# The shared expert's products move into the first routed block, and the rest of it into a later one

## The chip, the cores and the metric

The kernel runs on one core of a Trainium2 chip. The metric is the device time of one execution in microseconds, the median of several runs. The core has five engines that run side by side and are tied by semaphores: TensorE (PE, the matrix products), VectorE (DVE), ScalarE (ACT), GpSimd (POOL) and SyncE (SP), which here issues the DMAs that bring the weights from memory.

## The reference

One decoder layer for 256 tokens of width 1024. The first half (a convolution branch, an attention branch and an output projection) is not touched by the change. The second half is a mixture of experts: 64 routed experts of which each token uses 8, and one shared expert that every token uses.

```
def moe_ffn(h, w_router, router_bias, w_gu, w_down, w_sh_gu, w_sh_down):
    t = h.reshape(B * S, D)
    scores = jax.nn.sigmoid((t @ w_router).astype(f32))
    ...                                     # top 8 of 64, limited to 4 of 8 groups -> gates
        g, u = jnp.split(jnp.einsum('td,edf->tef', tc, w_gu), 2, axis=-1)
        return jnp.einsum('tef,efd->td', jax.nn.silu(g) * u * gc[..., None], w_down)
    ...
    sg, su = jnp.split(t @ w_sh_gu, 2, axis=-1)
    shared = (jax.nn.silu(sg) * su) @ w_sh_down
    return (routed + shared).reshape(B, S, D)
```

Everything is float32. An expert has a gate/up matrix of 1024 x 512 (2 MB) and a down matrix of 256 x 1024 (1 MB).

## The kernel before

**Blocks.** The routed experts are computed in blocks of 128 slots. Blocks 0, 1 and 2 take two fixed experts each, 64 slots for an expert; all later blocks take experts in the order of how many tokens chose them (the ranked blocks), with 1, 2 or 4 experts in a block. Tokens are gathered into a block's slots by products with a selection matrix (`moves`, L1523), and scattered back by products with its transpose (`combine`, L1710).

**One block on the engines.** In `experts` (L1790): 16 gate/up products (L1802; 32 with four experts in a block), silu on ScalarE (L1672), gating on VectorE (L1676), which also needs the gate column that VectorE makes from a small product (L1564, L1577), two transposes on TensorE (L1823), their copy on ScalarE (L1685), and the down products (L1849). VectorE scales their result (L1694), and it is scattered back a block later. ScalarE's first silu of a block needs the table of silu, which `activate` asks for when it comes to it; the table before it is that of the sigmoid.

**The shared expert.** `shared` (L1768) multiplies the two halves of the tokens, t = 0 and 1, with the shared gate/up matrix, 2 products for each of 8 row blocks k (L1784), first k = 0 to 3 for both halves (q = 0), then 4 to 7 (q = 1). Once the first routed block is prepared (the event `blk 0`) it stops until the event `static`, which block 3 sets after its gate/up products. When a half is complete, `shared_tail` (L1635) applies silu and the gating, two transposes (L1625), a copy (L1629) and the down products in two halves (L1647), scaled by VectorE (L1650) and added by GpSimd (L1653).

**The overflow chain.** `overflow` (L1443) finds the experts with more tokens than slots: small products (L1446, L1447, L1455, L1461, L1462) that go back and forth between TensorE and VectorE, then two transposes (L1474), a copy and products (L1479). Its list is read by every engine at the end (L1947); it is put into SP's queue as early as it fits.

**What sets the order.** All this is written as generators (fibers) which a planner (`Plan`, L49) runs while the kernel is built. Each `yield` names an engine and a cost, an event, or a buffer of a pool; the planner keeps a clock for each engine and lets that fiber go next that can start first, and of equals the one with the higher number in `PRIO` (L25). `shared`, `shared_tail` and `overflow` have 0 and fill what others leave. The result is one fixed order of instructions on each engine; at run time only semaphores decide when each starts. A change of one event can so move many instructions.

**The weights.** All loads are issued by SP, strictly in the order of `todo` (L252). A load needs a buffer of 1 MB (`fa` or `late_w`) and is put into the queue where the planner expects that buffer to be free; on the chip SP then waits for the products that last read it. The two down matrices of block 2 are in `late_w`; their buffers go to two of the four down matrices of block 3. The loads before these take the buffers of block 0 (in halves), of block 1 and of block 2's gate/up matrices.

Of the kernel before, what the change touches and what calls it, by code (L numbers as in the profile page):

```python
# [13 lines left out]
AF = mybir.ActivationFunctionType  # L14
# [173 lines left out]
def AP(n, table=None):  # L188
    return "A", 0.06 + 0.00082 * n, table
# [11 lines left out]
def tile_hybrid_block(ctx, tc, x, c, positions, w_ada, b_ada, norm1_g, w_in, conv_dw, conv_dw_b,  # L201
# [3 lines left out]
    nc = tc.nc  # L205
# [1280 lines left out]
    def evacuate(xt, f, p, p3, ns, b0):  # L1486
        for f2 in range(2):
            k = f + f2
            e = yield TS(ns) if not b0 and f % 4 == 0 else AP(ns)
            if e == "A":  # L1490
                nc.scalar.activation(xt[:, k, 0:ns], p3[:, f2, 0:ns], AF.Identity, bias=b2c[:, k:k + 1],  # L1491
                                     scale=a2c[:, k:k + 1])
            else:
                nc.vector.tensor_scalar(xt[:, k, 0:ns], p3[:, f2, 0:ns], a2c[:, k:k + 1], b2c[:, k:k + 1],
                                        op0=OP.mult, op1=OP.add)
        pl.put("bank", p)
        pl.set("xt", b0, f // 2)
# [90 lines left out]
    def gathers():  # L1588
        tables[0] = yield Get("pm")
        held = []  # L1590
        for t in range(2):
            pl.cur.prio = PRIO["gathers" if t else "compare"]
            yield pl.ev("rx", t)
            yield from compare(0, t, rxp[0])
            for q in range(2):
                yield pl.ev("xr", t, q)
            if t:
                pl.set("first_pm")
                opened(0, (yield Get("xt")))
            for f in range(0, K, 2):  # L1600
                if not t:
                    held.append((yield Get("bank")))
                yield MM(4 * 2 * P)
                p3 = moved(0, held[f // 2], f, (t,))
                if t:
                    pl.spawn(evacuate(pl.events["info", 0].whole, f, held[f // 2], p3, 2 * P, 0))
        for b in range(2):
            pl.set("blk", b)
        for b in range(2):
            yield from slots(b)  # L1610
# [22 lines left out]
    shared_left = [2]  # L1633

    def shared_tail(t, pg):  # L1635
        aT = yield from gate_up(pg, None)
        yield pl.ev("L", "sd", 0, 0)
        wd = loaded["sd", 0]
        yield max(wd.at)
        for i in (10, 11):  # L1640
            yield pl.ev("ada", i)
        for h in range(2):
            d = slice(h * 512, (h + 1) * 512)
            pd = yield Get("bank")
            yield MM(8 * 512)
            for f in range(2):
                nc.tensor.matmul(pd, aT[:, f], wd.k[f][:, d], start=(f == 0), stop=(f == 1))  # L1647
            tm = yield Get("tm2")
            yield TT(512)
            nc.vector.tensor_tensor(tm, pd, g2b[:, d], op=OP.mult)  # L1650
            pl.put("bank", pd)
            e = yield [GT(512), TT(512) + (None, 1.0)]
            (nc.gpsimd if e == "G" else nc.vector).tensor_tensor(x_sb[:, t, d], x_sb[:, t, d], tm, op=OP.add)  # L1653
            pl.put("tm2", tm)
        pl.put("aT", aT)
        shared_left[0] -= 1
        if not shared_left[0]:
            done(("sd", 0), 0)
            pl.put("o32", *(fa(80 + 2 * i, 512) for i in range(2)))
            pl.set("shared")  # L1660
# [107 lines left out]
    def shared():  # L1768
        w = None
        pgs = []  # L1770
        for q in range(2):
            for t in range(2):
                for k in range(4 * q, 4 * q + 4):
                    yield pl.ev("h2", t, k)
                    if not k:
                        pgs.append((yield Get("bank")))
                    yield pl.ev("L", "sg", 0, k // 2)
                    w = loaded["sg", 0]
                    yield w.at[k]
                    if pl.ev("blk", 0).t is not None:  # L1780
                        yield pl.ev("static")
                    for c_ in (slice(0, 256), slice(256, 512)):
                        yield MM(4 * 256)
                        nc.tensor.matmul(pgs[t][:, c_], h2T[:, k, t * P:(t + 1) * P], w.k[k][:, c_],  # L1784
                                         start=(k + c_.start == 0), stop=(k == K - 1 and c_.start > 0))
                if q:
                    pl.spawn(shared_tail(t, pgs[t]))
            done(("sg", 0), q)

    def experts():  # L1790
        for b, (kd, js) in enumerate(blocks):
# [53 lines left out]
            for f in range(2):  # L1845
                for h in range(2):
                    yield "P", 0.87
                    for e, o, m in tiles_of[kd]:
                        nc.tensor.matmul(pd[h][o:o + m], info.aT[:, f, o:o + m],  # L1849
                                         loaded["d", js[e]].k[f][:, h * 512:(h + 1) * 512],  # L1850
                                         start=(f == 0), stop=(f == 1))
            for j in js:
                done(("d", j), 0)
            pl.put("aT", info.aT)
# [146 lines left out]
```

## Time and profile before

| | |
|---|---|
| median of 3 runs | 818.3 us (818.0 to 819.95) |
| the profiled execution | 819.49 us, of it the span of the profile 817.7 us |
| PE busy | 766.1 us (94%) |
| DVE, ACT, POOL busy | 444.6, 324.9, 192.4 us |
| HBM read | 269.11 MB, 330 GB/s over the span |

The profile counts time from the start of the span. The first half of the layer ends at about 317 us; block 0's gate/up products begin at about 337 us, the ranked blocks at 389.55 us. In the rows a line number is that of the kernel before, a product of float32 is recorded as two MATMULs (x16 are eight products), the time behind the start is that of the group, and what stands in brackets is how long the engine stood idle before it and what released it. Matmul records overlap a little, so the distance from one group's start to the next one's says more than the recorded length. PEclk is the granted clock of TensorE, 1.00 being 2.4 GHz and 0.50 being 1.2 GHz.

### The profile page before, as it was taken

How to read it: one execution, taken by the hardware profiler on the slowest of the kernel's cores; microseconds unless marked ns; L12 is line 12 of the kernel's file. 1: busy time of each engine (PE TensorE's matmuls, PEld its weight loads, DVE VectorE, ACT ScalarE, POOL GpSimd, SP SyncE). 2: the span in 40 equal slices, each digit the busy share in tenths (PEclk: the TensorE clock that was granted, in tenths of full speed). 3: DMA queues.
4: the chain of work that ended last, by engine and by line, in shares of the span. 5: the costliest groups of instructions: out<-in, count | busy, mean ns of one | idle time of the engine just before them, and what ended most of it. 6: DMA issues, size and time to landing. Idle time of an engine off the chain costs nothing.

```text
span 817.7 us, 13180 instructions
## 1 busy us (share of the span) xinstructions
PE 766.1 (94%) x4759; PEld 469.8 (57%) x4759; DVE 444.6 (54%) x1035; ACT 324.9 (40%) x713; POOL 192.4 (24%) x246
## 2 busy tenths in 40 slices
PE   3999999899996999999999797999999999999997
PEld 2898777589784987545454141354464455444543
DVE  5458998999996677433433141344344344433443
ACT  4356656865759755223221021232232232232220
POOL 3003788888572693000002000000000000000000
PEclk9999999899997999989999898999999999999999
DMA  9998776546654676469999999999999999999993
GB/s 312 365 336 288 261 253 227 180 161 227 228 184 155 239 280 252 165 245 390 390 420 420 422 421 420 421 422 420 420 421 422 421 420 421 420 421 419 419 413 139
DMA packets 69883, 271.04 MB, mean 331 GB/s; under 512 B 6085, under 2 KB 15893, under 8 KB 46520
## 3 DMA queue, kind: packets, MB, share of 16 engines
q1 hardware_dynamic: 69464, 270.00, 84.9%
q8 instruction: 38, 0.62, 0.3%
q0 software_dynamic: 304, 0.16, 0.1%
q14 instruction: 29, 0.24, 0.1%
q10 hardware_dynamic: 48, 0.01, 0.0%
HBM read 269.11 MB, written 1.05 MB: 330 GB/s over the span
## 4 chain that ended last, share of the span: by engine, by line


## 5 line engine op out<-in xcount | busy, mean ns | idle before, releaser
L1802 PE MATMUL bank<-fa 128*32 128x512 f32 (+2 forms) x1048 | 203.7, 608 | 8.3 <-DMA fa<-in_w_exp_gu_dram 8.3
L1802 PEld LDWEIGHTS bank<-fa 128*32 128x32 f32 (+2 forms) x1048 | 60.3, 124 | 132.1 <-issue 107.3
L863 DVE SCALAR_TENSOR_TENSOR bank<-fa,tap,bank 128x256 f32<-128x256 f32 x232 | 112.9, 486 | 6.1
L1676 DVE SCALAR_TENSOR_TENSOR fa<-bank,gsc,h 128x256 f32<-128x256 f32 x28 | 13.5, 484 | 170.1 <-ACT h L1672 170.1
L1849 PE MATMUL bank<-fa 128*32 128x512 f32 (+1 forms) x496 | 83.9, 596 | 0.0
L1672 ACT ACTIVATE h<-bank 128x256 f32<-128x256 f32 x28 | 10.8, 385 | 179.7 <-PE bank L1802 179.7
L776 POOL TENSOR_TENSOR rb<-fa,rb 128x512 fp32r<-128x512 f32 x46 | 60.2, 1317 | 65.6 <-ACT rb L795 64.6
L1694 DVE TENSOR_TENSOR fa<-bank,fa 128x512 f32<-128x512 f32 x54 | 37.4, 692 | 65.5 <-PE bank L1849 62.7
L776 POOL TENSOR_TENSOR ra<-fa,ra 128x512 fp32r<-128x512 f32 x48 | 63.9, 1339 | 20.5 <-ACT ra L795 17.1
L1762 ACT CAST obs<-fa 128x512 fp32r<-128x512 f32 x54 | 33.4, 618 | 83.7 <-DVE fa L1694 83.7
L1719 DVE TENSOR_TENSOR fa<-fa,bank 128x512 f32<-128x512 f32 x108 | 66.7, 678 | 0.0
L1491 ACT ACTIVATE fa<-bank,b2c,a2c 128x256 f32<-128x256 f32 x108 | 53.6, 561 | 20.8 <-PE bank L1523 20.8
L795 ACT CAST ra<-fa 128x512 fp32r<-128x512 f32 x76 | 46.8, 622 | 37.0 <-PE bank L812 22.9
L1523 PE MATMUL bank<-ra 128*128 128x256 f32 x448 | 60.5, 288 | 0.0
L1710 PE MATMUL bank<-obs,ra 128*128 128x512 f32 x216 | 58.3, 412 | 0.0
L795 ACT CAST rb<-fa 128x512 fp32r<-128x512 f32 x68 | 42.0, 623 | 37.8 <-PE bank L812 22.4
L1802 PE MATMUL bank<-late_w,fa 128*32 128x512 f32 (+2 forms) x168 | 51.9, 627 | 4.1 <-DMA late_w<-in_w_exp_gu_dram 4.1
L1523 PEld LDWEIGHTS bank<-ra 128*128 128x128 f32 x448 | 55.6, 191 | 0.2
L1710 PEld LDWEIGHTS bank<-obs,ra 128*128 128x128 f32 x216 | 38.7, 188 | 28.8 <-issue 21.5
L811 PE MATMUL bank<-ra 128*128 128x256 f32 x160 | 47.8, 299 | 1.9 <-ACT ra L577 1.8
L1849 PEld LDWEIGHTS bank<-fa 128*32 128x32 f32 (+1 forms) x496 | 22.8, 119 | 41.1 <-issue 35.3
L811 PE MATMUL bank<-ra,rb 128*128 128x256 f32 x160 | 46.1, 288 | 0.0
(376 smaller groups left out, 1391.5 us busy)
## 6 DMA issues: line engine op xcount, KB each, us to landing
fa<-in_w_exp_gu_dram SPq DMA_DIRECT2D x100, 1024.0 KB, 19.8
fa<-in_w_exp_down_dram SPq DMA_DIRECT2D x50, 1024.0 KB, 19.8
fa<-in_w_ada_dram SPq DMA_DIRECT2D x24, 1024.0 KB, 7.9
fa<-in_w_in_dram SPq DMA_DIRECT2D x22, 1024.0 KB, 5.3
late_w<-in_w_exp_gu_dram SPq DMA_DIRECT2D x17, 1024.0 KB, 19.3
late_w<-in_w_exp_down_dram SPq DMA_DIRECT2D x12, 1024.0 KB, 6.8
fa<-in_w_exp_gu_dram SPq DMA_DIRECT2D x22, 512.0 KB, 9.4
fa<-in_w_in_dram SPq DMA_DIRECT2D x12, 512.0 KB, 9.4
```

Source lines behind the costliest of these rows:

```text
L776: (nc.gpsimd if e == "G" else nc.vector).tensor_tensor(hl[:, 1], w.k[k], hl[:, 0].bitcast(F32), op=OP.subtract)
L795: nc.scalar.copy(hl[:, 0], w.k[k])
L811: nc.tensor.matmul(o, hl[:, 0, mm], src_t[:, k, 0], start=(k == 0 and m % 2 == 0), stop=False)
L863: nc.vector.scalar_tensor_tensor(cv[:, m] if j == TAPS - 1 else acc, u_sb[:, m, j:j + T], tap[:, m, j:j + 1], acc, op0=OP.mult, op1=OP.add)
L1491: nc.scalar.activation(xt[:, k, 0:ns], p3[:, f2, 0:ns], AF.Identity, bias=b2c[:, k:k + 1], scale=a2c[:, k:k + 1])
L1523: nc.tensor.matmul(p3[:, f2, 0:ns], xr[:, a, t, (f + f2) * P:(f + f2 + 1) * P], tables[b0][:, t, 0:ns], start=(f2 + t + a == 0), stop=(f2 ...
L1694: nc.vector.tensor_tensor(o32, pd[h], g2b[:, h * 512:(h + 1) * 512], op=OP.mult)
L1710: nc.tensor.matmul(p, info.pT[:, t * P:(t + 1) * P], ob[a], start=(a == 0), stop=(a == 1))
L1719: nc.vector.tensor_tensor(x_sb[:, t, d], x_sb[:, t, d], p, op=OP.add)
L1762: nc.scalar.copy(ob[0], o32)
L1802: nc.tensor.matmul(pg[o:o + m], info.xt[:, k, o:o + m], loaded["g", js[e]].k[k], start=(k == 0), stop=(k == K - 1))
L1849: nc.tensor.matmul(pd[h][o:o + m], info.aT[:, f, o:o + m], loaded["d", js[e]].k[f][:, h * 512:(h + 1) * 512], start=(f == 0), stop=(f == 1))
```

## The change

Three edits. Silu's table is asked for at the end of `gathers`, by an activation of one element. `shared` no longer stops at `blk 0` but at a new event, `down 0`, set when block 0's down products are issued; until then it goes on. `shared_tail`, too, goes on if `down 0` is not yet set and otherwise waits for `static`.

```diff
--- before.py
+++ after.py
@@ -1604,6 +1604,8 @@
                 p3 = moved(0, held[f // 2], f, (t,))
                 if t:
                     pl.spawn(evacuate(pl.events["info", 0].whole, f, held[f // 2], p3, 2 * P, 0))
+        yield AP(1, "silu")
+        nc.scalar.activation(warm, iop, AF.Silu)
         for b in range(2):
             pl.set("blk", b)
         for b in range(2):
@@ -1633,6 +1635,8 @@
     shared_left = [2]
 
     def shared_tail(t, pg):
+        if pl.ev("down", 0).t is not None:
+            yield pl.ev("static")
         aT = yield from gate_up(pg, None)
         yield pl.ev("L", "sd", 0, 0)
         wd = loaded["sd", 0]
@@ -1777,7 +1781,7 @@
                     yield pl.ev("L", "sg", 0, k // 2)
                     w = loaded["sg", 0]
                     yield w.at[k]
-                    if pl.ev("blk", 0).t is not None:
+                    if pl.ev("down", 0).t is not None:
                         yield pl.ev("static")
                     for c_ in (slice(0, 256), slice(256, 512)):
                         yield MM(4 * 256)
@@ -1849,6 +1853,7 @@
                         nc.tensor.matmul(pd[h][o:o + m], info.aT[:, f, o:o + m],
                                          loaded["d", js[e]].k[f][:, h * 512:(h + 1) * 512],
                                          start=(f == 0), stop=(f == 1))
+            pl.set("down", b)
             for j in js:
                 done(("d", j), 0)
             pl.put("aT", info.aT)
```

The lines of the kernel after are shifted: the shared products are L1788, its transposes L1627, its down products L1651; the gate/up products L1806, the block's transposes L1827, the down products L1853, the silu L1676, the scaling L1698.

The order of instructions on TensorE at the head of block 0 (`bank_76` and `bank_79` hold the shared sums of t = 0 and 1, `bank_75` the block's), before:

```order
L1416 MATMUL bank_78<-ident,fa 64x128 x2
L1802 MATMUL bank_75<-fa 64x512 x2
L1421 MATMUL bank_77<-fa 128x64 x2
L1802 MATMUL bank_75<-fa 64x512 x7
L1802 MATMUL bank_75<-late_w_3129,fa 64x512
```

and after:

```order
L1416 MATMUL bank_78<-ident,fa 64x128 x2
L1788 MATMUL bank_76<-fa 128x256 x2
L1421 MATMUL bank_77<-fa 128x64 x2
L1788 MATMUL bank_76<-fa 128x256 x2
L1806 MATMUL bank_75<-fa 64x512 x9
```

Four shared products of t = 0 (k = 6 and 7) stand ahead of the block's gate/up products, on both sides of L1421, which no longer stands among them.

TensorE, the tail of block 0, from the products for its gate columns on to its down products, before:

```order
L1564 MATMUL bank_80<-ra 128x4 x2
L1567 MATMUL bank_80<-ident,ra 128x128 x2
L1564 MATMUL bank_74<-ra 128x4 x2
L1567 MATMUL bank_74<-ident,ra 128x128 x2
L1446 MATMUL bank_73<-fa 64x1
L1447 MATMUL bank_73<-iop,fa 64x1
L1455 LDWEIGHTS trib
L1455 MATMUL bank_73<-ovb,trib 64x1
L1461 MATMUL bank_73<-fa 1x64
L1462 MATMUL bank_73<-ones,fa 1x1
L1823 MATMUL bank_75<-ident,fa 128x128 x2
L1849 MATMUL bank_78<-late_w,fa 64x512 x2
```

and after:

```order
L1564 MATMUL bank_80<-ra 128x4 x2
L1567 MATMUL bank_80<-ident,ra 128x128 x2
L1564 MATMUL bank_74<-ra 128x4 x2
L1567 MATMUL bank_74<-ident,ra 128x128 x2
L1788 MATMUL bank_79<-fa 128x256
L1827 MATMUL bank_75<-ident,fa 128x128 x2
L1788 MATMUL bank_79<-fa 128x256
L1853 MATMUL bank_78<-late_w,fa 64x512 x2
```

The overflow chain has left this place, and two shared products of t = 1 stand around the block's transposes.

TensorE, block 2, from its transposes to its down products, before:

```order
L1823 MATMUL bank_80<-ident,fa 128x128 x2
L1474 MATMUL bank_73<-ident,fa 64x128 x2
L1479 MATMUL bank_73<-fa 128x64 x2
L1523 MATMUL bank_78<-ra 128x256 x8
L1523 MATMUL bank_77<-ra 128x256 x8
L1564 MATMUL bank_80<-ra 128x8 x2
L1567 MATMUL bank_80<-ident,ra 128x128 x2
L1849 MATMUL bank_74<-late_w,fa 64x512 x2
```

and after, up to the overflow's transposes:

```order
L1827 MATMUL bank_80<-ident,fa 128x128 x2
L1788 MATMUL bank_79<-fa 128x256 x2
L1627 MATMUL bank_76<-ident,fa 128x128 x2
L1446 MATMUL bank_73<-fa 64x1
L1447 MATMUL bank_73<-iop,fa 64x1
L1651 MATMUL bank_78<-fa 128x512 x2
L1455 LDWEIGHTS trib
L1455 MATMUL bank_73<-ovb,trib 64x1
L1461 MATMUL bank_73<-fa 1x64
L1462 MATMUL bank_73<-ones,fa 1x1
L1651 MATMUL bank_77<-fa 128x512 x2
L1474 MATMUL bank_73<-ident,fa 64x128 x2
```

Behind these the order is as before (L1479, L1523 and so on to the down products, L1853). Two more shared products, the shared transposes, both halves of the shared down product for t = 0 and the whole overflow chain now stand between block 2's transposes and its down products. The rest of t = 1 stays behind block 3.

On ScalarE the table load moves from between the two casts of slot matrices (L1584) and block 0's silu to behind L1418, and the silu of block 0 and that of the shared half t = 0 move ahead of the casts. On VectorE block 0's gating moves to directly behind its gate column, ahead of the second one. On SP the load of the overflow's list moves from ahead of the loads into block 0's down buffers to behind the last weight; the order of the weights stays.

## Rows read from the trace of the kernel before

**Rows 1.** Stretches of the span: busy time by engine, granted clock, DMA share, GB/s
```profile
350.00:355.00 5.00, 4.94 (x14) 1.54 (x16) 0.23 (x1) 0.01 (x1) 0.00 (x0) 0.54 0.03 10
385.00:390.00 5.00, 5.00 (x30) 2.02 (x32) 1.98 (x8) 2.35 (x6) 0.00 (x0) 1.00 0.92 387
390.00:395.00 5.00, 5.00 (x52) 1.56 (x48) 1.68 (x3) 0.83 (x2) 0.00 (x0) 1.00 0.87 324
395.00:530.00 135.00, 121.61 (x686) 52.90 (x679) 40.57 (x86) 26.77 (x58) 5.09 (x4) 0.95 1.01 421
530.00:800.00 270.00, 269.95 (x1673) 131.85 (x1671) 109.63 (x236) 74.43 (x158) 0.00 (x0) 1.00 1.01 419
```

**Rows 2.** What TensorE waited for, 400 to 817 us: total, times, longest
```profile
PE bank L1802 <- DMA fa<-in_w_exp_gu_dram: 8.3, 8, 1.5
PE bank L1802 <- DMA late_w<-in_w_exp_gu_dram: 4.1, 3, 1.4
```

**Rows 3.** TensorE at 527 us: start, duration, line, tiles, idle before and releaser
```profile
527.64 0.64 PE L1802 MATMUL bank<-late_w,fa 128*64 128x512 f32 x1 [1.30 <-DMA late_w<-in_w_exp_gu_dram]
```

**Rows 4.** What SP's DMA queue waited for, 346 to 380 us
```profile
SPq L270 <- PE bank L1849: 14.1, 2, 7.9
...
SPq L1947 <- DVE fa L1469: 4.2, 1, 4.2
```

**Rows 5.** The same, 380 to 396 us
```profile
SPq L270 <- PE bank L1849: 8.5, 1, 8.5
```

**Rows 6.** SP's issues around block 2
```profile
389.65 0.90 SPq L270 DMA_DIRECT2D late_w<-in_w_exp_down_dram  x2
```

**Rows 7.** TensorE, tail of block 0
```profile
344.74 0.38 PE L1564 MATMUL bank<-ra 128*128 128x4 f32 x2
...
347.66 0.28 PE L1461 MATMUL bank<-fa 64*1 64x64 f32 x2 [0.53 <-DVE fa L1459]
...
348.86 0.70 PE L1823 MATMUL bank<-ident,fa 128*128 128x128 f32 x2 [0.89 <-DVE fa L1676]
350.06 5.89 PE L1849 MATMUL bank<-late_w,fa 128*64 128x512 f32 x16 [0.51 <-ACT fa L1685]
355.79 0.59 PE L1802 MATMUL bank<-fa 128*64 128x512 f32 x2
```

**Rows 8.** VectorE, tail of block 0
```profile
345.53 0.16 DVE L1577 SCALAR_TENSOR_TENSOR gsc<-bank,bmaskP 128x4 f32<-128x4 f32 x1 [5.96 <-PE bank L1567]
...
348.32 0.48 DVE L1676 SCALAR_TENSOR_TENSOR fa<-bank,gsc,h 128x256 f32<-128x256 f32 x1 [0.72 <-ACT h L1672]
```

**Rows 9.** ScalarE, tail of block 0
```profile
345.74 0.79 ACT L1584 CAST ra<-bank 128x256 fp32r<-128x256 f32 x2 [8.02 <-DVE gsc L1577]
346.53 1.28 ACT L1672 ACT_TABLE_LOAD   x1
...
349.64 0.37 ACT L1685 COPY fa<-bank 128x256 f32<-128x256 f32 x1 [1.43 <-PE bank L1823]
```

**Rows 10.** TensorE, block 2, from its transposes to block 3
```profile
381.97 0.38 PE L1474 MATMUL bank<-ident,fa 128*64 128x128 f32 x2
...
385.97 3.65 PE L1849 MATMUL bank<-late_w,fa 128*64 128x512 f32 x16
389.55 0.64 PE L1802 MATMUL bank<-fa 128*32 128x512 f32 x4
```

**Rows 11.** TensorE, shared expert where it stands now
```profile
420.75 3.72 PE L1784 MATMUL bank<-fa 128*128 128x256 f32 x16
...
429.37 0.39 PE L1625 MATMUL bank<-ident,fa 128*128 128x128 f32 x2
430.27 1.98 PE L1647 MATMUL bank<-fa 128*128 128x512 f32 x4 [0.51 <-ACT fa L1629]
432.09 0.39 PE L1625 MATMUL bank<-ident,fa 128*128 128x128 f32 x2
```

**Rows 12.** VectorE, scaling of a down product
```profile
388.81 0.69 DVE L1694 TENSOR_TENSOR fa<-bank,fa 128x512 f32<-128x512 f32 x1 [1.75 <-PE bank L1849]
```

## The prediction

> **What bounds the kernel now.** I read the stretches of the span first (clock and DMA share by stage), then what the tensor engine waits for, then what the DMA queue on SP waits for, and last the instructions around block 0 and block 2. The reader is to see two things. From about 395 us to 800 us the DMA engines are full: share 1.01 both in 395 to 530 and in 530 to 800 [rows 1]. And up to 527.64 us the tensor engine waits for expert weights, eleven times, 12.4 us together [rows 2]; the last of these waits ends at 527.64 us [rows 3], and after it the engine is busy for 269.95 of the 270 us from 530 to 800 [rows 1]. So the end of the kernel is tied to one landing: when the weight of 527.64 us lands, some 290 us of gapless matmul work follow (817.7 - 527.6). Since the DMA stream has no hole between 395 and 530, that landing moves by exactly as much as the stream at 395 us moves. Matmul work that is taken out of 395 to 527 us, or put into it, changes nothing: it is paid out of the 12.4 us of waiting.
>
> What places the stream at 395 us are the holes before it. It stands still in 350 to 355 us (share 0.03), and it runs dry once more around 390 us, for about 0.4 + 0.65 us (shares 0.92 and 0.87) [rows 1]. Both times SP, which issues its DMAs strictly in order, waits for the tensor engine to give a buffer back by the down products of a block (L1849): 14.1 us in two waits, for blocks 0 and 1, and 8.5 us in one, for block 2 [rows 4, 5]. The two loads released by block 2 are issued at 389.65 us [rows 6], right when its down products, begun at 385.97, end (block 3 begins at 389.55) [rows 10]. Behind them in SP's queue stands everything else. So the question about the change is: at what time do the down products of block 2 end? The DMA has no work in hand there.
>
> **The change, part by part.** I follow the tensor engine from block 0 to that point.
>
> Four shared products before and beside L1421, ahead of block 0's gate and up products. Eight such products took 3.72 us, 0.46 us each [rows 11]: +1.86 us. No wait stands there in the old order that they could fill, so they count in full. They also delay the half loads that SP issues as block 0 goes on, but these still end before block 0's down products release the next pair.
>
> The tail of block 0, from its last gate/up product to its first down product: 344.74 to 350.06, 5.32 us now [rows 7]. In it stand two casts (0.79), the table load (1.28), silu, the gating on DVE at 348.32, and the overflow chain on both engines [rows 7 to 9]. After the change the table is long loaded (ACT idles 8.02 us before these casts [rows 9]), silu follows the products at once, and the gating waits for the gate column: 0.79 us from 344.74 to 345.53, then 0.24 for it, 0.48 for the gating, 0.06 to the transposes, 1.57 us [rows 7, 8]. One product of 0.46 us fills most of that. The transposed copy on ACT (0.37) now stands behind the second cast, which waits for the second gate column behind the gating on DVE: 1.75 + 0.39 + 0.37 and 0.05 of handing over, so the down products start 2.6 us after 344.74. That is -2.72 us. The bounds are 2.3 us (the engine's own work: transposes and products) and the old 5.32.
>
> The clock. Between 346 and 350.06 the engine stood idle several times (0.53, 0.89 and 0.51 us in [rows 7]), and the granted clock in 350 to 355 is 0.54 [rows 1], close to the lower level of 1.2 GHz. The down products of block 0 take 5.73 us to the next product (350.06 to 355.79), those of block 2, at full clock, 3.58 us (385.97 to 389.55) [rows 7, 10]: 2.15 us. With the waits filled I take all of it as won, -2.15 us (the other bound is 0). The Trainium skill ("TensorE: Matmul & The Clock Gate", section "HAM oscillation — how this bites in real kernels") says that idle gaps between groups of matmuls put the engine back to its lower clock; the trace agrees here.
>
> So block 0's down products end 1.86 - 2.72 - 2.15 = -3.0 us earlier. SP's wait for the overflow list (L1947, 4.2 us [rows 4]) goes to the end of SP's queue; it stood in the shadow of the wait for block 0 and wins nothing. Block 1 and block 2's gate and up products keep their order, so they come 3.0 us earlier too.
>
> The work now put between block 2's transposes and its down products. Today that stretch is 381.97 to 385.97, 4.0 us [rows 10]. Added are: two shared products, 0.93; the shared transposes and the wait for their copy on ACT, 0.90 (429.37 to 430.27); the first half of the shared down product, 1.82 (430.27 to 432.09) [rows 11]; the overflow chain, whose products 1446 and 1447 fit into the wait just counted; then L1461 and L1462 behind DVE; and the second half of the shared down product, 1.82. The chain costs more here than at block 0: on DVE the scaling of the shared half (0.69, as L1694 [rows 12]) now stands between the copies that L1461 waits for. At block 0 the wait before L1461 was 0.53 us [rows 7]; here it is 0.16 of the product's end, 0.69 and about 0.55, 1.4 us, and then 0.31 for the pair. Sum: 0.93 + 0.90 + 1.82 + 1.40 + 0.31 + 1.82 = +7.2 us. The bounds are 5.3 us, if both waits vanish, and 9.3, if the clock falls there too (2.15 as at block 0).
>
> Net at the release of block 2: -3.0 + 7.2 = +4.2 us. The DMA, which has run 3.0 us earlier, is dry 3.0 us earlier and is fed 4.2 us later: its hole grows from 1 us to about 8. The shared work that is missing after 400 us in turn (some 8 us: 1.86 + 0.92 + 0.93 + 0.90 + 3.64) only lengthens the waits for DMA. The forecast is therefore +4.2 us. The profiled execution took 819.49 us with a span of 817.7; its span would become 821.9. The median of the runs, 818.3, lies 1.2 us below that execution, and the shift is put on it: 822.5 us. With the ends of all terms together the net runs from 2.0 (1.86 - 3.02 - 2.15 + 5.3) to 11.2 (1.86 + 9.3, nothing won at block 0); I stay at the values of the nearest rows.
>
> **The rivals.**
> Faster: block 0's gain goes through. If the DMA still has loads in hand when block 2 is late, the 3.0 us that the 14.1 us waits of SP lose are all that counts: 818.3 - 3.0 = 815.3 us. For it speaks that the largest hole is the one at 350 us. Against it: SP's 8.5 us wait and the share of 0.92 in 385 to 390 say that nothing is in hand at 390 us, so the sign turns where the stretch in block 2 grows by more than 3.0 us. The Trainium skill ("Perfetto Trace Analysis", "Optimization Strategies" under DMA performance) says to keep the matmul engine as highly used as possible and to go after what makes it wait; by that rule filling block 0's waits would bring this rival's time. The trace speaks against the rule here, since the engine's later waits (12.4 us) are for DMA.
> No change: the stretch in block 2 costs what block 0 gives, within 1.5 us, since the waits for ACT and DVE overlap more than I let them (5.3 us and a gain of 3.0 to 3.8): about 820 us.
> Deeper loss: the clock falls in block 2's new stretch, with its waits of 0.4, 1.1 and 0.5 us, or does not stay up in block 0: 2.15 us more, 824.7 us.
> That the products don't move as said is excluded by the order of instructions.
>
> **How the numbers follow.** Forecast 0.66 (own range 820.4 to 824.0), faster 0.12, no change 0.12, deeper loss 0.10. A measurement of this kernel can tell about 0.3% (2.5 us) from no change. Slower by more than that, above 820.8: 0.9 of the forecast and all of the deeper loss, 0.69. Faster, below 815.8: 0.12 with a little of the rest, 0.13. Within: 0.18. The range of 817.8 to 825.0 holds the forecast, the no-change case and most of the deeper loss, and leaves out the faster one.
>
> **What would show it.** Block 0's down products at full clock, starting near 349.2 us, block 1's products near 352.8 (355.79 now). In block 2's stretch, the two halves of the shared down product, a wait of about 1 us before L1461 of the overflow chain, and the down products some 4 us later than now. SP's pair of loads issued near 393.9 us and a DMA hole of about 8 us before 395. The last wait for a weight ending near 531.8, and no more waits behind it. If the DMA share is 1.0 from 385 on, or block 2's stretch takes under 7 us in all, the forecast is wrong and the faster rival holds; a granted clock below 0.8 between 383 and 396 would be the deeper loss.

## The result and the profile after

| | before | after |
|---|---|---|
| median (runs) | 819.1 us (818.0 to 821.5, 4) | 829.9 us (827.0 to 830.3, 4) |
| profiled execution / span | 819.49 / 817.7 us | 829.69 / 827.9 us |
| ratio after to before, 95% interval | | 1.012 (1.0086 to 1.0153) |

The changed kernel is slower, as forecast, but by 10.8 us between the medians where +4.2 was forecast; the time lies above the range. Ratios, here and below, leave out one execution of b2_plus that took 910.6 us at a granted clock of 0.81.

The stretches of the span after the change (columns as in [rows 1]):

```profile
350.00:355.00 5.00, 4.90 (x28) 2.51 (x28) 1.54 (x9) 1.50 (x4) 0.00 (x0) 1.00 0.95 374
385.00:390.00 5.00, 2.95 (x10) 1.18 (x9) 3.24 (x10) 0.00 (x0) 1.26 (x1) 0.88 0.99 416
390.00:395.00 5.00, 4.54 (x21) 2.71 (x20) 1.17 (x3) 0.60 (x2) 1.27 (x1) 0.78 0.03 11
395.00:400.00 5.00, 5.00 (x30) 2.07 (x32) 1.91 (x8) 2.35 (x6) 0.00 (x0) 1.00 0.00 0
405.00:540.00 135.00, 117.39 (x660) 48.43 (x653) 38.77 (x83) 26.10 (x56) 2.53 (x2) 0.95 1.01 421
540.00:810.00 270.00, 269.96 (x1672) 131.40 (x1669) 109.64 (x236) 74.35 (x158) 0.00 (x0) 1.00 1.01 419
```

The hole in the DMA at 390 us, 1 us long before, now lasts 10 us (0.03 and 0.00), and the clock falls where it begins (0.88 and 0.78 in 385 to 395 us). From 405 us on the DMA is full as it was, and TensorE is less busy than before (117.39 of 135 us, 121.61 before), with longer waits for weights, 16.6 us instead of 12.4, as forecast for the shared work that is missing there. What TensorE waits for there, and the last of these waits [rows 2, 3]:

```profile
PE bank L1806 <- DMA fa<-in_w_exp_gu_dram: 10.9, 10, 1.4
PE bank L1806 <- DMA late_w<-in_w_exp_gu_dram: 4.3, 3, 1.4
PE bank L1853 <- DMA fa<-in_w_exp_down_dram: 1.4, 2, 0.7
```

```profile
537.66 3.65 PE L1806 MATMUL bank<-fa 128*64 128x512 f32 x14 [1.31 <-DMA fa<-in_w_exp_gu_dram]
```

SP's wait for the down products from 346 us to the release, and the pair of loads released by block 2 [rows 4 to 6]:

```profile
SPq L270 <- PE bank L1853: 32.1, 3, 18.3
```

```profile
399.71 0.90 SPq L270 DMA_DIRECT2D late_w<-in_w_exp_down_dram  x2
```

The longest wait has grown from 8.5 to 18.3 us. The pair is 10.06 us later than before (389.65), the last wait 10.02 us, the span 10.2 us: the three go together, as the forecast had it. So the question is only why the pair is 10 us late and not 4.

TensorE, block 0 [rows 7]:

```profile
340.32 0.38 PE L1416 MATMUL bank<-ident,fa 128*64 128x128 f32 x2
...
350.16 0.38 PE L1564 MATMUL bank<-ra 128*128 128x4 f32 x2
...
351.10 0.60 PE L1788 MATMUL bank<-fa 128*128 128x256 f32 x2
351.71 0.51 PE L1827 MATMUL bank<-ident,fa 128*128 128x128 f32 x2
...
352.73 3.65 PE L1853 MATMUL bank<-late_w,fa 128*64 128x512 f32 x16
356.22 1.03 PE L1806 MATMUL bank<-fa 128*64 128x512 f32 x4
```

L1416 stands ahead of everything that the change moves, and it starts at 340.32 us; before it started at 336.68:

```profile
336.68 0.38 PE L1416 MATMUL bank<-ident,fa 128*64 128x128 f32 x2
```

TensorE's recorded instructions up to it are the same ones in the same order in both profiles. So 3.64 us are lost where no instruction of TensorE has moved. From L1416 on block 0 does what was forecast: the down products begin 2.57 us after L1564 (5.32 before, 2.6 forecast), run at full clock (3.49 us to block 1, 5.73 before), and block 1 begins 15.90 us after L1416 (19.11 before): 3.2 us won, 3.0 forecast.

TensorE, block 2, from its transposes to block 3 [rows 10, 11]:

```profile
382.18 0.39 PE L1827 MATMUL bank<-ident,fa 128*128 128x128 f32 x2
382.41 1.03 PE L1788 MATMUL bank<-fa 128*128 128x256 f32 x4
383.27 0.39 PE L1627 MATMUL bank<-ident,fa 128*128 128x128 f32 x2
...
384.18 1.98 PE L1651 MATMUL bank<-fa 128*128 128x512 f32 x4 [0.20 <-ACT fa L1631]
386.09 0.19 PE L1455 MATMUL bank<-ovb,trib 64*64 64x1 bf16 x1
388.34 0.27 PE L1461 MATMUL bank<-fa 64*1 64x64 f32 x2 [2.05 <-DVE fa L1459]
388.45 0.19 PE L1462 MATMUL bank<-ones,fa 64*1 64x1 f32 x2
388.56 3.64 PE L1651 MATMUL bank<-fa 128*128 128x512 f32 x4
391.99 0.47 PE L1474 MATMUL bank<-ident,fa 128*64 128x128 f32 x2
...
396.03 3.65 PE L1853 MATMUL bank<-late_w,fa 128*64 128x512 f32 x16
```

Before, the stretch began with

```profile
381.74 0.39 PE L1823 MATMUL bank<-ident,fa 128*128 128x128 f32 x2
```

From the transposes to the down products it now takes 13.85 us (before 381.74 to 385.97, 4.23): +9.6 where +7.2 was forecast. Two rows stand out: the wait of 2.05 us before L1461, and the second half of the shared down product, 3.43 us from start to start where the first took 1.91. The wait is explained by VectorE and GpSimd side by side:

```profile
386.99 1.30 DVE L1459 TENSOR_SCALAR fa<-iot,fa 64x64 f32<-64x64 f32 x1
```

```profile
386.97 1.26 POOL L1657 TENSOR_TENSOR fa<-fa 128x512 f32<-128x512 f32 x1 [56.90 <-DVE fa L1457]
```

L1459 on 64x64 numbers takes 1.30 us, and it ends 0.06 us after GpSimd's sum, which began 0.02 us earlier. That the one causes the other is tested below (dve_add).

### The profile page after: what moved, and what is told of

Its sections match the earlier page's. It is cut to its first block, busy times and chain, and to the rows that moved or that the text cites. A ratio compares the mean times of both kernels' runs of the same rounds, so it can differ in the third digit from the quotient of the medians.

```text
span 827.9 us, 13173 instructions
## 1 busy us (share of the span) xinstructions
PE 773.1 (93%) x4759; PEld 473.1 (57%) x4759; DVE 446.2 (54%) x1035; ACT 325.4 (39%) x714; POOL 191.9 (23%) x246
## 4 chain that ended last, share of the span: by engine, by line
## 5 line engine op out<-in xcount | busy, mean ns | idle before, releaser
L1806 PE MATMUL bank<-fa 128*32 128x512 f32 (+2 forms) x1040 | 200.5, 614 | 11.0 <-DMA fa<-in_w_exp_gu_dram 10.9
L1806 PEld LDWEIGHTS bank<-fa 128*32 128x32 f32 (+2 forms) x1040 | 58.9, 126 | 136.5 <-issue 106.9
L1676 ACT ACTIVATE h<-bank 128x256 f32<-128x256 f32 x28 | 10.8, 384 | 195.5 <-PE bank L1806 195.5
L1853 PE MATMUL bank<-fa 128*32 128x512 f32 (+2 forms) x504 | 82.2, 596 | 1.4 <-DMA fa<-in_w_exp_down_dram 1.4
L1698 DVE TENSOR_TENSOR fa<-bank,fa 128x512 f32<-128x512 f32 x54 | 37.3, 692 | 67.5 <-PE bank L1853 64.9
L1523 PE MATMUL bank<-ra 128*128 128x256 f32 x448 | 60.5, 288 | 0.0
L1523 PEld LDWEIGHTS bank<-ra 128*128 128x128 f32 x448 | 55.6, 191 | 0.2
L811 PE MATMUL bank<-ra 128*128 128x256 f32 x160 | 48.5, 303 | 1.9 <-ACT ra L577 1.8
L1853 PEld LDWEIGHTS bank<-fa 128*32 128x32 f32 (+2 forms) x504 | 22.5, 119 | 44.9 <-issue 36.5
L812 PE MATMUL bank<-ra 128*128 128x256 f32 x160 | 46.6, 291 | 0.0
L813 PE MATMUL bank<-ra 128*128 128x256 f32 x160 | 46.4, 290 | 0.0
```

What stands on the lines that cost most here:

```text
L811: nc.tensor.matmul(o, hl[:, 0, mm], src_t[:, k, 0], start=(k == 0 and m % 2 == 0), stop=False)
L812: nc.tensor.matmul(o, hl[:, 0, mm], src_t[:, k, 1], start=False, stop=False)
L813: nc.tensor.matmul(o, hl[:, 1, mm], src_t[:, k, 0], start=False, stop=last)
L1523: nc.tensor.matmul(p3[:, f2, 0:ns], xr[:, a, t, (f + f2) * P:(f + f2 + 1) * P], tables[b0][:, t, 0:ns], start=(f2 + t + a == 0), stop=(f2 ...
L1806: nc.tensor.matmul(pg[o:o + m], info.xt[:, k, o:o + m], loaded["g", js[e]].k[k], start=(k == 0), stop=(k == K - 1))
L1853: nc.tensor.matmul(pd[h][o:o + m], info.aT[:, f, o:o + m], loaded["d", js[e]].k[f][:, h * 512:(h + 1) * 512], start=(f == 0), stop=(f == 1))
```

## The experiments

The theory: the end is the release of block 2's down buffers plus a constant, and what the kernel itself sets is the time from L1416 to that release. The rivals: TensorE's work counts wherever it stands; or the changed kernel is slow by itself before 340 us. All runs at a glance, by the names used below (one profile each; granted clock of 5 to 330 us; start of L1416; the pair of loads behind block 2; ratio to the kernel before, with its interval):

| run | PEclk | L1416 | pair | pair - L1416 | span | span - pair | ratio |
|---|---|---|---|---|---|---|---|
| before | 0.96 | 336.68 | 389.65 | 52.97 | 817.7 | 428.1 | |
| before_again | 0.96 | 335.97 | 388.70 | 52.73 | 816.9 | 428.2 | 0.998 (0.996 to 1.000) |
| after | 0.94 | 340.32 | 399.71 | 59.39 | 827.9 | 428.2 | 1.012 (1.009 to 1.015) |
| after_again | 0.94 | 341.07 | 400.40 | 59.33 | 828.2 | 427.8 | 1.009 (1.007 to 1.011) |
| after_third | 0.95 | 338.49 | 397.85 | 59.36 | 826.2 | 428.3 | 1.007 (1.005 to 1.010) |
| b2_plus | 0.95 | 338.71 | 398.43 | 59.72 | 826.4 | 428.0 | 1.010 (1.009 to 1.012) |
| b4_plus | 0.95 | 337.32 | 390.20 | 52.88 | 818.4 | 428.2 | 1.001 (0.999 to 1.002) |
| tail_late | 0.94 | 340.30 | 396.05 | 55.75 | 823.9 | 427.9 | 1.004 (1.003 to 1.006) |
| dve_add | 0.95 | 338.65 | 398.36 | 59.71 | 826.3 | 427.9 | 1.010 (1.007 to 1.012) |
| filler | 0.95 | 338.24 | 396.30 | 58.06 | 824.3 | 428.0 | 1.006 (1.004 to 1.009) |
| no_silu | 0.96 | 336.42 | 395.39 | 58.97 | 823.6 | 428.2 | 1.006 (1.004 to 1.008) |
| best1 | 0.95 | 339.12 | 389.41 | 50.29 | 818.5 | 429.1 | 1.000 (0.998 to 1.001) |
| x5 | 0.94 | 340.42 | 389.37 | 48.95 | 819.7 | 430.3 | 0.998 (0.997 to 1.000) |
| x6 | 0.96 | 336.04 | 384.57 | 48.53 | 812.6 | 428.0 | 0.995 (0.993 to 0.997) |

### Work in block 2 against work in block 4

Runs b2_plus and b4_plus:

```diff
             for j in js:
                 yield pl.ev("L", "d", j, 0)
                 yield max(loaded["d", j].at)
+            if b == 2:                      # b2_plus; b == 4 in b4_plus
+                for _ in range(8):
+                    nc.tensor.matmul(pd[0], ident, g2b[:, 0:512], start=True, stop=True)
```

> The kernel before, with eight products of 128x512 that are used for nothing put between block 2's copy and its down products (written over by these): 8 x 0.91 = 7.3 us at full clock, nothing else moved. Theory A (the end hangs on the release of block 2's down buffers): SP's pair goes from 389.65 to 396.9 and the time rises by 7.3 us, to 825 to 826.5. Rival (the DMA has loads in hand, or the 12.4 us in which TensorE waits for weights later take it up): less than 3 us more, 818 to 821.

> The kernel before, with the same eight products of 128x512 (7.3 us) as in the experiment on block 2, now ahead of block 4's down products, at some 418 us, where the DMA is full. Theory A (the DMA stream is the limit from the release of block 2 on): the 12.4 us that TensorE waits for weights up to 527 us shrink by 7 us and the time does not move, 819 to 821.5 us. Rival (the end is the sum of TensorE's work from block 0 on, or the later release of block 4's buffers opens a hole in the DMA): the time rises by 4 to 7.3 us, to 824 to 828.

In block 2 the work costs its full price: 59.72 us from L1416 to the pair, 6.8 more than before (the products' 7.0 less small gains), and the span follows. The time is 1.0% longer, some 8 us where 7.3 was expected; in the profiled execution L1416 was 2 us later than in that of the kernel before. In block 4 the same eight products cost nothing:

```profile
417.63 7.03 PE L1847 MATMUL bank<-fa,ident 128*128 128x512 f32 x16
```

The expected way was half right. The waits for DMA up to 545 us are 10.2 us instead of 12.4; the rest fits a clock that stayed up more (0.98 in 390 to 530 us, 0.95 before: 0.03 of 140 us is 4.2 us), in one profile of each. The rival that all work counts falls.

### Block 2's stretch without the shared tail

Run tail_late:

```diff
     def shared_tail(t, pg):
-        if pl.ev("down", 0).t is not None:
-            yield pl.ev("static")
+        yield pl.ev("static")
```

> The changed kernel, with both shared tails waiting for block 3's event: the shared transposes and down products of t = 0 leave block 2; two shared products and the overflow chain stay between block 2's transposes and its down products. Theory A (end = release of block 2's down buffers plus a constant): the stretch in block 2, 13.6 us in the kernel after, falls to 4.0 + 0.93 + 0.4 + some 1.5 of waits in the chain = 6 to 8 us; with the 3 us won at block 0 the release lies within 1.5 us of the kernel before, and so does the time: 817 to 821 us. Rival (the kernel after is slow because of the clock in its first half or the work moved behind 400 us, not because of block 2): the time stays within 2 us of the kernel after, 827 to 830.

The time fell, as only the theory has it (ratio to the kernel before 1.004; after_again, measured beside it, 1.009), but less than expected: 825.2 us where 817 to 821 was expected, and 3.6 us less from L1416 to the pair. The stretch was to fall to 6 to 8 us and is still 10.1 (382.23 to 392.37). TensorE in it:

```profile
382.23 0.39 PE L1826 MATMUL bank<-ident,fa 128*128 128x128 f32 x2
...
383.42 0.27 PE L1446 MATMUL bank<-fa 64*64 64x1 f32 x2
...
386.36 0.30 PE L1474 MATMUL bank<-ident,fa 128*64 128x128 f32 x1 [0.96 <-DVE fa L1471]
387.01 0.30 PE L1474 MATMUL bank<-ident,fa 128*64 128x128 f32 x1 [0.36 <-DVE fa L1471]
387.77 0.66 PE L1479 MATMUL bank<-fa 64*128 64x64 f32 x4 [0.46 <-ACT fa L1476]
388.35 3.50 PE L1523 MATMUL bank<-ra 128*128 128x256 f32 x16
391.65 0.42 PE L1564 MATMUL bank<-ra 128*128 128x8 f32 x2
...
392.37 3.65 PE L1852 MATMUL bank<-late_w,fa 128*64 128x512 f32 x16
```

The overflow chain alone takes 4.9 us (383.42 to 388.35), 2.9 of it waiting, and behind the waits the gathers take 3.30 us (granted clock 0.59 in 388 to 392 us) where they take 2.02 at full clock. I had priced its waits at 1.5 us: the six operations of VectorE before L1474 (L1467 to L1471) lay under other work before.

### VectorE beside GpSimd

Run dve_add:

```diff
-            e = yield [GT(512), TT(512) + (None, 1.0)]
+            e = yield TT(512)
```

> The changed kernel, with the sums of the shared expert (L1656) on VectorE instead of GpSimd; with it the second half of the shared down product moves ahead of L1461. Theory A (the wait of 2.05 us before L1461 comes from L1459 on VectorE, 1.30 us long beside GpSimd's sum and 0.25 us at block 0, and the gaps then let the clock fall): L1459 takes 0.25 us again, the wait before L1461 is gone, the clock stays up; from L1416 to SP's pair 55 to 57.4 us instead of 59.4, and the time 2 to 4 us under the kernel after, 824 to 826.5. Rival (VectorE, with two sums of some 0.6 us more, is later for the scaling and the chain than GpSimd's slowing made it): 59 us or more from L1416 to the pair, 828 us or more.

Half of it held. VectorE:

```profile
385.86 0.24 DVE L1459 TENSOR_SCALAR fa<-iot,fa 64x64 f32<-64x64 f32 x1
```

and TensorE behind it:

```profile
388.68 0.30 PE L1474 MATMUL bank<-ident,fa 128*64 128x128 f32 x1 [1.94 <-DVE fa L1471]
...
390.82 3.51 PE L1523 MATMUL bank<-ra 128*128 128x256 f32 x16
```

With GpSimd silent L1459 takes 0.24 us: its 1.30 us came from GpSimd's sum, in all four profiles where the two began together (the three of the kernel after, and no_silu below). The Trainium skill ("SBUF — State Buffer", "SBUF: two separate sides") says that GpSimd shares a pair of ports with some operations of VectorE (those in a two-port mode or with two inputs in SBUF) as an exclusive lock that whoever starts first keeps for its whole instruction; the 1.30 us fit that, and so does VectorE's copy L1481 out of a bank, which in the profile of after ran beside GpSimd's second sum (393.01 to 394.28 us) in 0.29 us, no longer than without it (0.29 in tail_late). But nothing was won: the two sums, now on VectorE, and the scaling delay L1471, TensorE waits 1.94 us there instead, and from 390 us on the clock falls (0.52 in 391 to 394). The rival holds for the time (59.71 us to the pair, 828.1 us).

### The wait and the clock

Run filler:

```diff
         nc.tensor.matmul(p[0:NE, 0:1], trib[0:NE, 0:NE], ovb, start=True, stop=True)      # L1455
+        for _ in range(4):
+            nc.tensor.matmul(p[:, 256:512], ident, g2b[:, 0:256], start=True, stop=True)
```

> The changed kernel with four more products of 128x256 (0.46 us each at full clock, used for nothing) between L1455 and L1461, that is in the 2.05 us in which TensorE waits for L1459 in block 2's stretch. In both profiles of the kernel after the granted clock goes to 0.5 right behind that wait (from 388.8 us on) for 3.4 us, and the second half of the shared down product takes 3.43 us instead of the 1.9 of the first half. Theory A (the idle wait costs twice, once itself and once by the clock): the products fit into the wait, the clock stays at 1.00 up to the down products, the second half takes 1.9 us; block 2's stretch falls from 13.85 to some 12.3 us in spite of 1.84 us more work, L1416 to the pair 57.8 us instead of 59.4. Rival (the clock falls for another reason, or the products cost what they take): 13.85 to 15.7 us, 59.4 us or more from L1416 to the pair.

TensorE in the stretch:

```profile
384.11 1.99 PE L1457 MATMUL bank<-fa,ident 128*128 128x256 f32 x8
386.63 0.27 PE L1463 MATMUL bank<-fa 64*1 64x64 f32 x2 [0.52 <-DVE fa L1461]
386.74 0.19 PE L1464 MATMUL bank<-ones,fa 64*1 64x1 f32 x2
386.86 1.98 PE L1653 MATMUL bank<-fa 128*128 128x512 f32 x4
```

With 1.9 us of useless work put in, the stretch became 1.3 us shorter (12.54 us, 58.06 to the pair): the second half of the shared down product takes 1.8 us again. That is what the theory expected, but it isn't proof that the wait made the clock fall. The run also changes a second thing: VectorE's copy ahead of L1459 (L1461 in this run's lines) now waits for the added products, so that it starts after GpSimd's sum has ended and takes 0.25 us again. The next run, no_silu, keeps the wait of 2.05 us as it was:

```diff
-        yield AP(1, "silu")
-        nc.scalar.activation(warm, iop, AF.Silu)
         for b in range(2):
             pl.set("blk", b)
```

> The changed kernel without the early table load: with it the four shared products ahead of block 0 go, and seven stand in block 0's tail instead (some 3.2 us of work), while ScalarE makes its casts and loads the table there; block 2's stretch is nearly that of the kernel after. Theory A (filled waits keep the clock up, and the table load is then hidden behind products): from L1416 to block 1's first gate and up product 16 to 17 us (19.1 in the kernel before, 15.9 in the kernel after), block 0's down products at full clock (3.5 us); to the pair 59.5 to 61 us, and the time 828 to 830. Rival (the early table load is what shortens block 0): 18 us or more to block 1, 61 or more to the pair, 830 to 832.

```profile
385.72 0.27 PE L1461 MATMUL bank<-fa 64*1 64x64 f32 x2 [2.05 <-DVE fa L1459]
385.83 0.19 PE L1462 MATMUL bank<-ones,fa 64*1 64x1 f32 x2
385.94 1.98 PE L1649 MATMUL bank<-fa 128*128 128x512 f32 x4
```

The wait of 2.05 us is there, and the clock stayed at 1.00, so the stretch is 12.68 us. Behind the wait, in after and in no_silu (columns as in [rows 1]):

```profile
388.00:391.00 3.00, 2.66 (x7) 1.23 (x8) 1.66 (x8) 0.00 (x0) 0.23 (x1) 0.63 0.67 279
```

```profile
386.00:389.00 3.00, 2.54 (x11) 1.24 (x10) 2.07 (x8) 0.37 (x1) 0.26 (x1) 1.00 0.28 117
```

The pair comes 58.97 us after L1416 and the time is 826.5 us, both a little below what was expected (59.5 to 61, 828 to 830). The Trainium skill ("TensorE: Matmul & The Clock Gate", "HAM oscillation — how this bites in real kernels") says that idle gaps between groups of matmuls put the engine back to its lower clock, with an example of longer waits than these; in the three profiles of the kernel after the clock fell behind the gap, here it did not behind the same gap. When such a gap costs the 1.6 us stays open.

For block 0 this run says that filled waits keep the clock up: 16.66 us from L1416 to block 1 (19.11 before), with the table load still there. The tail itself is hardly shorter (344.48 to 349.60, 5.12 us; 5.32 before), but eight shared products fill it, and the down products behind it take 3.48 us instead of 5.73. With the table early, two products in the tail and none ahead of the block (x5, below) it is 14.21.

### Is the changed kernel late before 340 us?

> The changed kernel once more, unaltered. In its first profile TensorE was 3.64 us late already at 340 us, before any instruction has moved: its clock stood at the lower level twice as long around 170 us and once more around 202 us. Theory A (the release of block 2's down buffers places the end; the early 3.6 us is a matter of the execution): the runs scatter over about 826 to 830.5 us as before, and a profile whose clock drops fewer times before 300 us has L1416 near 336.7 and SP's pair behind block 2 near 396, one with the same drops 340.3 and 399.7. Rival B (the early lateness belongs to the changed kernel): every profile has it, and every run lies 10 us above the kernel before, at 828 to 831.

> The changed kernel a third time, unaltered. Its ten runs so far fall into two heaps, four at 825.4 to 827.0 us and six at 829.7 to 830.3, and both profiles are of the upper heap: 37.5 and 40.9 us at the lower clock before 330 us, L1416 at 340.3 and 341.1, one more drop of 3.4 us in block 2's stretch. Theory A: L1416 follows the time at the lower clock before 330 us, as it did in the eleven other profiles of every kernel (336.0 at 23.8 us, 337.3 at 30.6, 338.7 at 34.1, 340.3 at 37.5), the release of block 2 comes 59.4 us later if the clock drops in its stretch, 57.8 if not, and the span is that plus 428.0. Rival (the changed kernel is late before 340 us by itself): L1416 at 340 or later again.

> The kernel before once more, for a second profile of it. So far every profile of a kernel with the table loaded early has L1416 at 339.1 to 341.1 us, the one of the kernel before at 336.68, one with eight more products in block 2 at 338.71. Theory A: the time of L1416 is a matter of the execution (how long TensorE's clock stands at its lower level before 300 us), and the time from L1416 to SP's pair of loads behind block 2 is what the kernel sets: 53.0 us here (52.97 in the first profile), and the span is that pair's time plus 428.0. Rival B: the kernel before has its L1416 at 336.7 always, and is then at 817.7 us of span again.

Over all fourteen profiles L1416 follows the granted clock of the first 330 us: 336.0 to 336.7 us at 0.96, 337.3 to 339.1 at 0.95, 340.3 to 341.1 at 0.94. b2_plus, whose order up to block 2 is that of the kernel before, had 338.71, and x6, with the early table load, 336.04. So L1416 can be late without the change and early with the early table load, and after_third's 338.49 is what the rival excludes; the 3.64 us are put down to the executions. What the kernel sets, from L1416 to the pair, is 59.33 to 59.39 us in three profiles against 52.73 to 52.97: 6.4 us. Over 17 executions the median of the kernel after is 828.0 us; the kernel before had 819.1, 820.7 and 820.5 beside them. That is 7.5 us or more, so about 1 us is left over.

All executions together bear this out, since the span of every one is on record, and not only of those with a profile. For the kernel before, 90 (those beside after_again, before_again, no_silu and after_third, and before_again itself) lie between 815.5 and 822.3 us with a median of 819.0; for the kernel after, 17 lie between 822.2 and 828.5 with a median of 826.2. The mean granted clock is 0.968 in both. Taken that span less pair and pair less L1416 are in all of them what the profiles show (481.0 us together before, 487.5 after), L1416 would start at 334.5 to 341.3 us before (median 338.0) and at 334.7 to 341.0 after (median 338.7). This is an estimate; by it the kernel before has the same spread as the kernel after, and what is left over is some 0.7 us. Over the profiles alone the kernels with the early table load are later (nine have L1416 at 339.2 us in the mean, the five others at 337.0), and whether they meet the lower clock a little more often is not settled.

### A version that keeps the gain

The runs best1, x5 and x6 keep both shared tails behind block 3 (as tail_late) and start the overflow chain at an event, with `PRIO` 9.9:

```diff
     def overflow():
+        yield pl.ev("down", 0)      # best1; "act", 1 in x5; "down", 1 in x6
         p = yield Get("bank")
```

x5 and x6 also set the events `blk` before the table load, so that the four products ahead of block 0 go:

```diff
-        yield AP(1, "silu")
-        nc.scalar.activation(warm, iop, AF.Silu)
         for b in range(2):
             pl.set("blk", b)
+        yield AP(1, "silu")
+        nc.scalar.activation(warm, iop, AF.Silu)
```

> The changed kernel, with both shared tails waiting for block 3's event and the overflow chain waiting for block 0's down products and then going first: its seven small products stand between block 1's gate and up products and in its combination, and block 2's stretch holds nothing but its own work. Theory A: block 0 gives its 3.0 us, block 2's stretch is 0.4 to 0.8 us shorter than the 4.0 us of the kernel before (the chain's two last pairs leave it), block 1 grows by about 1.3 us of small products; the release comes 2 to 3 us earlier than in the kernel before, the end too: 815 to 817 us at equal clock in the first half. Rival (the DMA still has work in hand, or the work that is missing later counts): no gain, 818 us or more.

> The changed kernel, with (1) the table load behind the events of blocks 0 and 1, so that no shared products stand ahead of block 0's gate and up products, (2) both shared tails behind block 3, (3) the overflow chain in block 1, among the gathers that follow its transposes and its down products. Theory A: from L1416 to the release of block 2's pair 48 to 49 us (52.97 before, 50.3 with the chain among block 1's gate and up products, which cost 2.0 us there). The DMA hole of 1 us at 390 is then closed, and the gain beyond it depends on the holes before (2 us in 355 to 360, 0.65 in 370 to 375): the time falls by 2 to 4.5 us against the kernel before, to 816 to 818.5. Rival (the DMA stream from block 0's release on is all that counts by then, and it is no shorter): the same as the kernel before, 820 to 821.

> The kernel with no shared products ahead of block 0 and both shared tails behind block 3, now with the overflow chain waiting for block 1's down products, so that it stands among block 2's gate and up products. In the version with the chain in block 1 the release of block 2 came 4.0 us earlier than before (48.95 us from L1416), but the time hardly moved: the DMA stood still in 372 to 375 us (3.4 us, 0.8 to 0.9 in the kernel before) until block 1's down buffers came free at 374.1, and 0.9 MB more than before was still to be loaded at the release of block 2. Theory A (the last of the DMA's holes places the end, and it was block 1's by then): block 1's down products end 31 to 31.5 us after L1416 (33.7 there, 36.1 in the kernel before), the hole in front shrinks to about 1 us, the pair of block 2 comes at 49 to 49.5, and the time falls to 3.5 us under the kernel before: 816.5 to 818 us. Rival (the holes before 360 us or the amount of loads place it): 819 to 820, as with the chain in block 1.

best1 and x5 bring the pair 2.7 and 4.0 us nearer to L1416 and hardly win (820.2 and 819.1 us, where 815 to 817 and 816 to 818.5 were expected), and here the constant breaks: span less pair is 429.1 and 430.3. At the release of block 2 some 0.6 and 0.7 MB more than before were still to be loaded (the sizes of the DMA packets that end after it), since the DMA had stood still earlier, at the release of block 1. At the 420 GB/s of the full stream that is 1.4 and 1.7 us, roughly the 1.0 and 2.2 by which the constant grew. A stretch of x5, and the same place in x6:

```profile
371.00:376.00 5.00, 5.00 (x26) 1.92 (x26) 2.46 (x5) 1.60 (x3) 0.00 (x0) 1.00 0.38 117
```

```profile
366.00:371.00 5.00, 5.00 (x28) 1.61 (x24) 2.88 (x7) 1.24 (x2) 0.00 (x0) 1.00 0.82 298
```

In x5 the chain's last pieces stood between block 1's down products, which ended 33.7 us after L1416; in x6 they end at 31.2, and that hole is short again (0.82, 0.84 before). SP's pair in x6:

```profile
384.57 0.90 SPq L270 DMA_DIRECT2D late_w<-in_w_exp_down_dram  x2
```

It comes 48.53 us after L1416, the constant is 428.0 again, and the time is 0.5% below the kernel before (817.0 us beside 822.4; ratio 0.9949, 0.9928 to 0.9970). From L1416 to the end of the span it takes 476.5 us, x5 479.2, best1 479.3, the kernel before 480.9 to 481.0. This version beats both kernels, by little but clear of the noise.

## Why the prediction was off

- **The end hangs on block 2's release.** Right, to 0.3 us over the twelve profiles in which block 2's release is the last hole; shown by b2_plus and b4_plus. The rival "faster" had it that the DMA has loads in hand at 390 us; it had none.
- **Block 0, -3.0 us.** Right: 3.2. The four products ahead cost 1.8 (15.99 us to block 1 in best1, 14.21 in x5; forecast 1.86), the tail is 2.57 long (2.6), the clock gave 2.2 (2.15).
- **The step that failed: the work put into block 2, "0.93 + 0.90 + 1.82 + 1.40 + 0.31 + 1.82 = +7.2 us".** Measured from start to start: 0.86 + 0.91 + 1.91 + 2.25 + 0.22 + 3.43 = 9.6. Four terms hold. "L1461 and L1462 behind DVE", 1.40, was 2.25: I added durations of VectorE alone and did not look who runs beside it; GpSimd's sum, which starts on the same scaling, stood in rows at 430 us and came along. The second half, 1.82, was 3.43: the clock fell. That was my rival "deeper loss", with a chance of 0.10 and 824.7 us. By the segment alone (819.5 + 6.4 - 1.2 = 824.7) its figure came out, but partly by luck: it put all 2.15 us on the clock, and measured were 1.6 for the clock and 0.85 for the wait, less 0.2 at block 0. What makes the clock fall behind this wait in one kernel and not in another stays open.
- **The level.** I put the shift on the median of three runs, 1.2 us below the profiled execution. That execution had one of the fastest first parts of all: L1416 at 336.68, while it lies between 336.0 and 341.1 over the profiles, and in the profile of after it was 3.64 us later. My range had room for the terms of the sum and none for this spread, as wide as the whole forecast. With the sum put right the forecast would have been 824.7 us, just inside the range; of the other 5 us up to the measured 829.9, nearly all are the 3.64 and the 1.2.
- **The signs named in advance.** Block 0's down products at full clock: yes. Start near 349.2: 349.09, less the 3.64. SP's pair near 393.9: 399.71. A wait of about 1 us before L1461: 2.05. A DMA hole of 8 us: 10. A granted clock below 0.8 between 383 and 396: 0.78. The last wait near 531.8: 537.66, and no wait for DMA behind it.

## What to carry to other kernels

When the DMA is full from some release on, look for the last release that it stands still for: work in front of it costs its whole length, the same work behind it nothing, and when that hole closes, the hole before it can be the next bound (x5 against x6 here). A chain of tiny operations that goes back and forth between two engines is priced by its waits at the new place, with everything that the other engines do there, and not by its busy time. Before a change is compared at half a per cent, find a point of the trace ahead of the change and measure from there.

## What was not expected of the hardware

- A VectorE operation of 0.25 us took 1.30 us beside a GpSimd sum of 1.26 us that began 0.02 us earlier, and 0.24 without it.
- The same kernel starts one and the same instruction at 338.49, 340.32 or 341.07 us, with the granted clock of the first 330 us at 0.95 or 0.94.
- The same wait of 2.05 us was followed by a clock of 0.5 in three profiles of one kernel and by 1.00 in another kernel's; the table load (1.28 us) was followed by its activation 0.01 us later.
